# Expert rows by indirect DMA for the first 128 tokens of a mixture layer, up products for the other 384

## The chip, the cores and the metric

The kernel runs as one program on one core of a Trainium2 chip. The metric is the device time of that program in microseconds (us), the median of several runs. The engines are TensorE (PE, with its weight loads shown apart as PEld), VectorE (DVE), ScalarE (ACT), GpSimd (POOL) and SyncE (SP). SP and POOL also issue the transfers between device memory and SBUF.

## What is computed

The program is a two-layer diffusion-style block, then a block with sparse and dilated attention, then a product-key expert layer ("peer"). Only the expert layer is touched. For 512 tokens of 1024 features it computes:

```
q   = (xt @ w_q).reshape(T, H, 2, 64)                 # H = 8 heads
s   = einsum('thcd,cnd->thcn', q, subkeys)            # 2 x 128 subkeys
s1, i1 = top_k(s[:, :, 0], 16);  s2, i2 = top_k(s[:, :, 1], 16)
sc, ci = top_k(s1[..., :, None] + s2[..., None, :], 16)   # of 256 candidates
idx = e1 * 128 + e2                                   # 16 experts of 16384 for each head
g   = softmax(sc)
a   = einsum('cd,chkd->chk', x, u[idx])               # u, v: 16384 x 1024
out = einsum('chk,chkd->cd', gelu(a) * g, v[idx])
```

So each token has 128 experts (8 heads of 16). The kernel before does not pick rows of u at all: it multiplies every token with all 16384 rows of u, and the weights g, spread over a dense table of 16384 experts by 512 tokens that is zero except at the chosen ones, do the picking.

## The kernel before, in words

Numbers are float32. Each product on TensorE is made of three: weights and activations are each split into a high part in a reduced form of float32 (fp32r) and the rest (`hi`, `lo`), and hi*hi, lo*hi and hi*lo are summed in PSUM (`mm3`, line 322). A tile of weights of 128 outputs comes by DMA from SP's queue (`wunit`, line 282), ACT writes `wh` (line 276), DVE writes `wl` (line 277). `lin2` (line 1096) runs the 24 products of one such tile, 8 chunks of features by 3, each with 512 tokens as moving columns.

The expert layer is `peer`. Its parts, in the order in which the code names them:

- the queries and scores: 8 tiles of `wpq`, then the scores of head h are copied to `SCO` (line 1629).
- `route(b)`, b = 0 to 3, for 128 tokens each: on DVE, the best 16 of 128 scores for each head and half (lines 1639 to 1643), the best 16 of 50 candidates, softmax (ACT for the exponential), and the two expert indices e1 and e2 (lines 1680 to 1699). Three transposes on PE (line 1704) put them and the weights on partitions by pair.
- `weights(tb, share)`, tb = 0 to 31, for 16 tokens each: groups of four tokens. DVE makes two one-hot tables (line 1719); ACT scales one of them by g, high part and low part, in eight small operations (line 1728), or in one group of three of the last block DVE does it in two (line 1725). Four products of 256 columns (line 1732) give, for each token, the 128x128 table of its expert weights, high part and low part next to each other; ACT copies the low parts (line 1735), DVE adds (line 1736) into `gst`. After 16 tokens `gst` goes to the table `G` in device memory from POOL's queue (line 1738).
- `up(e, ahead)`, e = 0 to 127: the product of one tile of 128 rows of u with all 512 tokens (`lin2`), gelu on ACT (line 1763), and, when it is made ahead of its use, a store to device memory (`GA`, line 1766).
- the down part, 16 groups of 8 tiles: `gt`, the weights of 1024 experts for all tokens, comes from `G` (line 1781), the gelu tiles come back from `GA` (line 1787), DVE multiplies them (line 1791), ACT and DVE split them into `hid` (lines 1794, 1795), and eight `lin2` with tiles of v (2048 + 1024 products in all) are added to the output (line 1799).

The code writes an interleaving by hand: `routing()` yields the time that each step is thought to take on DVE and ACT, and whenever 3.62 us have gathered on either, one `up` is written (lines 1769 to 1776). `route(b + 1)` is written between the groups of `weights` of block b. By that count 121 of the 128 up products are written during the routing, and seven in the first group of the down part. A planner of the framework then fixes each engine's order from the written order and from what it takes to be ready; at run time each engine runs its list in order.

One-hot tables and scaled tables have two buffers (`NOH`), split weights three (`NWH`), PSUM tiles of 1024 columns two (`acc`).

Of the kernel before, what the change touches and what calls it, by code (L numbers as in the profile page):

```python
# [5 lines left out]
F32 = mybir.dt.float32  # L6
# [64 lines left out]
NOH = 2  # L71
# [7 lines left out]
SHARE = 3  # L79

# [102 lines left out]
def pack2(i, o):  # L183
# [33 lines left out]
    o["pu"] = i["peer_u_2"].reshape(128, 128, 8, 128).transpose(1, 3, 2, 0)  # L217
    o["pv"] = i["peer_v_2"].reshape(128, 16, 8, 8, 128).transpose(1, 3, 0, 2, 4)
# [25 lines left out]
class K:  # L244
# [26 lines left out]
    def split(self, raw, shape):  # L271
        """hi, lo of raw"""
# [12 lines left out]
    def take(self, key, hold=False):  # L285
        """the next weights of the plan, the ones behind them on their way; held ones stay until they are dropped"""
# [12 lines left out]
    def drop(self, w):  # L299
        """a held one that is used for the last time"""  # L300
        self.held -= 1
        self.refill(1)
        return w
# [13 lines left out]
    def mm3(self, outs, w, x, start, stop):  # L317
        """outs: psum aps; w: (hi, lo) stationary; x: per out (hi, lo) moving."""
# [20 lines left out]
    def ones_mean(self, src, n, dim):  # L339
        """mean over features of src [128, n] (sum over partitions / dim), as psum [128, n]"""  # L340
# [23 lines left out]
    def setup(self):  # L364
# [4 lines left out]
        # gains times -1/2, the weights of the gated convolution times 1/2  # L369
# [26 lines left out]
    def load_xc(self):  # L396
        """the context's tokens, three feature chunks to a tile"""
# [36 lines left out]
    def adv(self, n=1000):  # L434
        """n steps of the first of the generators that run beside the tasks"""
# [25 lines left out]
    def mod_group(self, l, g, ws):  # L461
        """columns 256 g to 256 g + 256 of the modulation of layer l"""
# [15 lines left out]
    def mods(self, todo):  # L478
        """closures for the groups (layer, group) of todo; a group's weights are loaded behind the group before it"""
# [8 lines left out]
    def tick(self, upto=1000):  # L488
        """one more group of modulations, upto that many in all"""
# [4 lines left out]
    def mod_fold(self, l, j, gname, plus_one, k0, k1):  # L494
        """[128, k1 - k0, 2]: -gain / 2 * (mod_j (+1))"""
# [1374 lines left out]
```

## Time and profile before

| | us |
|---|---|
| median of 3 runs | 3798.35 (3797.68 to 3798.63) |
| the profiled execution, first to last instruction | 3799.5 |
| routing, weights and up products (2322 to 3098.8) | 776.8 |
| down part (3098.8 to the end) | 700.7 |

| engine, whole span | busy us | share |
|---|---|---|
| PE | 3700.0 | 97% |
| DVE | 2464.8 | 65% |
| ACT | 1749.5 | 46% |
| POOL | 159.3 | 4% |

The stage limits are read from the first and last starts of instructions: the products of `hid` start at 3098.8. Consecutive products on PE overlap in the records, so the pace of a kind is the distance between starts, not the duration of one. The same holds for DVE and ACT, where one instruction's end overlaps the next one's start by about 0.1 us.

### The profile page before, as it was taken

How to read it: one execution, taken by the hardware profiler on the slowest of the kernel's cores; microseconds unless marked ns; L12 is line 12 of the kernel's file. 1: busy time of each engine (PE TensorE's matmuls, PEld its weight loads, DVE VectorE, ACT ScalarE, POOL GpSimd, SP SyncE). 2: the span in 40 equal slices, each digit the busy share in tenths (PEclk: the TensorE clock that was granted, in tenths of full speed). 3: DMA queues.
4: the chain of work that ended last, by engine and by line, in shares of the span. 5: the costliest groups of instructions: out<-in, count | busy, mean ns of one | idle time of the engine just before them, and what ended most of it. 6: DMA issues, size and time to landing. Idle time of an engine off the chain costs nothing.

```text
span 3799.5 us, 52788 instructions
## 1 busy us (share of the span) xinstructions
PE 3700.0 (97%) x19762; PEld 3052.0 (80%) x19762; DVE 2464.8 (65%) x4950; ACT 1749.5 (46%) x3452; POOL 159.3 (4%) x317
## 2 busy tenths in 40 slices
PE   8998999999999999999999999999999999999999
PEld 5867788888877878887778878778888888888887
DVE  5966644444788655555776568999666855555554
ACT  5256531111446732233565544767777743322232
POOL 0000000000000000000001100000000011111110
PEclk9999999999999999999999999999999999999999
DMA  6430331222341233334331233455555565665553
GB/s 209 129 106 12 122 117 62 61 66 63 105 147 51 67 117 95 94 97 138 115 99 62 93 111 106 156 168 176 178 178 178 195 218 189 201 205 187 190 186 114
DMA packets 155248, 490.28 MB, mean 129 GB/s; under 512 B 18368, under 2 KB 24832, under 8 KB 150768
## 3 DMA queue, kind: packets, MB, share of 16 engines
q1 hardware_dynamic: 128368, 374.48, 30.9%
q0 software_dynamic: 26624, 112.43, 8.7%
q8 instruction: 156, 2.56, 0.3%
q14 instruction: 100, 0.82, 0.1%
HBM read 408.86 MB, written 74.71 MB: 127 GB/s over the span
## 4 chain that ended last, share of the span: by engine, by line
PE 85%; DVE 9%; ACT 2%; DMA 2%; issue 1%; SPq 0%; POOL 0%; ACTq 0%; DVEq 0%; POOLq 0%
PE b L322 56%; PE a L322 19%; PE b L917 2%; DVE wl L277 1%; PE b L467 1%; PE a L1732 1%; PE b L568 1%; PE b L906 1%; PE b L1419 1%; PE b L1365 1%; DMA mraw<-in_wmod_dram 1%; DVE gst L1736 1%; PE a L1125 0%; PE b L1507 0%; PE b L1174 0%
## 5 line engine op out<-in xcount | busy, mean ns | idle before, releaser
L276 ACT CAST wh<-raw 128x1024 fp32r<-128x1024 f32 (+2 forms) x531 | 547.3, 1031 | 1365.7 <-PE b L322 811.3
L322 PE MATMUL b<-hs,wh 128*128 128x512 f32 x2624 | 823.6, 395 | 4.4 <-ACT hs L1092 4.4
L277 DVE TENSOR_TENSOR wl<-raw,wh 128x1024 fp32r<-128x1024 f32 (+2 forms) x531 | 635.7, 1198 | 171.7 <-ACT wh L276 159.1
L322 PE MATMUL b<-hid,wh 128*128 128x512 f32 x2048 | 630.7, 389 | 0.0
L322 PEld LDWEIGHTS b<-hs,wh 128*128 128x128 f32 x2624 | 487.5, 190 | 107.7 <-ACT hs L1092 5.3
L322 PE MATMUL b<-hs,wl 128*128 128x512 f32 x1312 | 516.2, 393 | 1.1 <-DVE wl L277 1.1
L322 PEld LDWEIGHTS b<-hid,wh 128*128 128x128 f32 x2048 | 384.4, 188 | 80.2 <-DVE hid L1795 0.3
L322 PE MATMUL b<-hid,wl 128*128 128x512 f32 x1024 | 398.3, 389 | 0.0
L322 PE MATMUL b<-hh,wh 128*128 128x256 f32 (+1 forms) x1160 | 364.7, 351 | 3.7 <-DVE V L840 2.2
L322 PE MATMUL a<-hh,wh 128*128 128x512 f32 (+1 forms) x1144 | 354.7, 348 | 9.5 <-DVE y L1046 7.2
L322 PE MATMUL b<-hl,wh 128*128 128x256 f32 (+1 forms) x1160 | 356.3, 344 | 0.3 <-DVE hl L534 0.3
L322 PE MATMUL b<-hh,wl 128*128 128x256 f32 (+1 forms) x1160 | 355.7, 344 | 0.0
L322 PE MATMUL a<-hh,wl 128*128 128x512 f32 (+1 forms) x1144 | 350.2, 344 | 1.5 <-DVE wl L277 1.5
L322 PE MATMUL a<-hl,wh 128*128 128x512 f32 (+1 forms) x1144 | 349.9, 343 | 0.3 <-DVE hl L534 0.3
L322 PEld LDWEIGHTS b<-hs,wl 128*128 128x128 f32 x1312 | 248.4, 189 | 53.7 <-DVE wl L277 1.5
L322 PEld LDWEIGHTS b<-hh,wh 128*128 128x128 f32 x1160 | 200.5, 189 | 44.0 <-issue 4.7
L322 PEld LDWEIGHTS a<-hh,wh 128*128 128x128 f32 x1144 | 197.0, 188 | 44.3 <-issue 14.0
L322 PEld LDWEIGHTS b<-hl,wh 128*128 128x128 f32 x1160 | 201.0, 189 | 30.5 <-issue 1.2
L322 PEld LDWEIGHTS b<-hid,wl 128*128 128x128 f32 x1024 | 192.2, 188 | 39.9
L322 PEld LDWEIGHTS a<-hl,wh 128*128 128x128 f32 x1144 | 197.3, 188 | 31.8 <-issue 2.5
L322 PEld LDWEIGHTS b<-hh,wl 128*128 128x128 f32 x1160 | 200.4, 189 | 27.7 <-issue 1.1
L322 PEld LDWEIGHTS a<-hh,wl 128*128 128x128 f32 x1144 | 196.9, 188 | 30.3 <-DVE wl L277 2.3
(412 smaller groups left out, 5424.1 us busy)
## 6 DMA issues: line engine op xcount, KB each, us to landing
raw<-in_w_dram SPq DMA_DIRECT2D x134, 512.0 KB
raw<-in_pu_dram SPq DMA_DIRECT2D x128, 512.0 KB
raw<-in_pv_dram SPq DMA_DIRECT2D x128, 512.0 KB
raw<-in_win_dram SPq DMA_DIRECT2D x64, 512.0 KB
G<-gst POOLq DMA_DIRECT2D x32, 1024.0 KB, 4.9
gt<-G POOLq DMA_DIRECT2D x16, 2048.0 KB, 13.9
mraw<-in_wmod_dram SPq DMA_DIRECT2D x82, 384.0 KB
GA<-ga SPq DMA_DIRECT2D x121, 256.0 KB
```

The source lines that it names most:

```text
L276: nc.scalar.copy(hi, raw)
L277: nc.vector.tensor_tensor(lo, raw, hi, op=OP.subtract)
L322: nc.tensor.matmul(o, w[wi], xx[xi], start=start and xi == 0 and wi == 0, stop=stop and wi == 1)
L467: nc.tensor.matmul(p[j:j + 32, 0:256], self.cs[:, k, :], ws[k], start=k < 4, stop=k >= 4, tile_position=(0, j))
L568: nc.tensor.matmul(p[:, :w], self.ones[1024], s, start=k == 0, stop=k == 7)
L906: nc.tensor.transpose(p[:, j * 128:j * 128 + 128], Ps[e][:, kc * 128:kc * 128 + 128], self.eye)
L917: nc.tensor.matmul(o[pr, c % 2 * 128:c % 2 * 128 + 128], V[i][:, kc, pr], PT[e * nkb + kc], start=kc == 0, stop=kc == nkb - 1, tile_positi ...
L1365: nc.tensor.transpose(p[:, j * 128:j * 128 + 128], src, self.eye)
L1419: nc.tensor.matmul(o[row], V[kb][:, 128 * b + 64 * g:128 * b + 64 * g + 64], PT[kb][2 * g + b], start=False, stop=kb == qb and b == 1, til ...
L1732: nc.tensor.matmul(p[:, i * 256:i * 256 + 256], A[:, i], W[:, i].rearrange("p j e -> p (j e)"), start=True, stop=True)
L1736: nc.vector.tensor_tensor(gst[:, :, t8:t8 + 4].rearrange("p e t -> p t e"), q[:, :, 0], lo, op=OP.add)
```

## The change

For the first 128 tokens the up products are no longer made with all experts. After `route(0)` the flat expert index of each of the 128 pairs of each token is kept in `IDX`; `gather()` reads, for pair j, one row of u for each of the 128 tokens (128 rows of 4 KB, one indirect DMA on POOL's queue), and DVE multiplies that tile with the tokens (`XT`, token-major) and sums along the features into one column of `AU`. That is 128 DMAs and 128 DVE instructions of 128x1024. Three row buffers are used (`NGU`). Then gelu of `AU`, times g, and the result takes the place of g in the dense table of block 0.

The up products run on the other 384 tokens only. The order of the blocks becomes 1, 2, 3, 0, with `route(0)` and `route(1)` first, rows written alternately with the steps of `route(2)` and `route(3)`, the other rows beside and after the weights of block 3, and the weights of block 0 last, since they need `AU`.

In `weights` the high and low parts are now summed in PSUM: eight products of 128 columns for four tokens, where there were four of 256, and one ACT copy of 128x1024 for eight tokens, where there were two ACT copies of 128x512 and two DVE additions. In the down part the first 128 columns of a tile are copied from `gt` by ACT, and DVE multiplies the other 384.

```diff
+NGU = 3
+    o["un"] = i["peer_u_2"]
-    def lin2(self, ap, hs, shape=(128, 8, 128)):
+    def lin2(self, ap, hs, shape=(128, 8, 128), n=S):
-        p = self.acc1()
+        p = self.acc1()[:, :n]
...
+            if b == 0:
+                nc.vector.scalar_tensor_tensor(IDX, e12[:, 0], 128.0, e12[:, 1], op0=OP.mult, op1=OP.add)
+                nc.vector.tensor_copy(E0, e12)
+                nc.vector.tensor_copy(G0, gz)
+            else:
+                by_pair(b, e12, gz)
...
+        def gather():
+            ru = fr.enter_context(self.tc.tile_pool(name="ru", bufs=1))
+            AU = ru.tile([128, 128], F32, name="au")
+            XT = ru.tile([128, D], F32, name="XT")
+            U = {}
+            def issue(j):
+                U[j] = self.t("ug", [128, D], bufs=NGU, pool=ru)
+                nc.gpsimd.indirect_dma_start(out=U[j], out_offset=None, in_=a["un"],
+                                             in_offset=bass.IndirectOffsetOnAxis(ap=IDX[:, j:j + 1], axis=0))
+            for j in range(NGU - 1):
+                issue(j)
+            p = self.acc()
+            for k in range(8):
+                x = self.t("xs", [128, 128], bufs=2, pool=ru)
+                nc.vector.tensor_tensor(x, hs[k][0][:, :128].bitcast(F32), hs[k][1][:, :128].bitcast(F32), op=OP.add)
+                nc.tensor.transpose(p[:, k * 128:k * 128 + 128], x, self.eye)
+            nc.scalar.copy(XT, p)
+            yield 1500
+            for j in range(128):
+                u = U.pop(j)
+                nc.vector.tensor_tensor_reduce(u, u, XT, 1.0, 0.0, OP.mult, OP.add, AU[:, j:j + 1])
+                if j + NGU - 1 < 128:
+                    issue(j + NGU - 1)
+                yield 1150
+            nc.scalar.activation(AU, AU, AF.Gelu_apprx_tanh)
+            nc.vector.tensor_tensor(G0, G0, AU, op=OP.mult)
+            by_pair(0, E0, G0)
...
-                for i in range(4):
-                    nc.tensor.matmul(p[:, i * 256:i * 256 + 256], A[:, i], W[:, i].rearrange("p j e -> p (j e)"), start=True, stop=True)
-                q = p.rearrange("p (t j e) -> p t j e", t=4, j=2)
-                lo = self.t("glo", [128, 4, 128], bufs=1, pool=rt)
-                nc.scalar.copy(lo, q[:, :, 1])
-                nc.vector.tensor_tensor(gst[:, :, t8:t8 + 4].rearrange("p e t -> p t e"), q[:, :, 0], lo, op=OP.add)
+                    for i in range(4):
+                        c = 128 * (t4 + i)
+                        for j in range(2):
+                            nc.tensor.matmul(p[:, c:c + 128], A[:, i], W[:, i, j], start=j == 0, stop=j == 1)
+                nc.scalar.copy(gst[:, :, t8:t8 + 8], p.rearrange("p (t e) -> p e t", t=8))
...
+            for ns in route(1):
+                yield ns, 0
+            r0.close()
+            rows = gather()
+            def beside(r):
+                for ns in r:
+                    yield ns
+                    yield next(rows, 0)
-            for b in range(4):
-                r = route(b + 1) if b < 3 else iter(())
+            for b in (1, 2, 3, 0):
+                r = beside(route(b + 1)) if b in (1, 2) else rows if b == 3 else iter(())
...
-            p = self.lin2(a["pu"][e], hs)
+            p = self.lin2(a["pu"][e], [(hi[:, 128:], lo[:, 128:]) for hi, lo in hs], n=S - 128)
...
-                nc.vector.tensor_tensor(gv, gv, gt[:, :, e, :], op=OP.mult)
+                n0 = 128 // TBW
+                nc.scalar.copy(gv[:, :n0], gt[:, :n0, e, :])
+                nc.vector.tensor_tensor(gv[:, n0:], gv[:, n0:], gt[:, n0:, e, :], op=OP.mult)
```

## Rows read from the trace of the kernel before

**Rows 1.** The page's head: span; engine, busy us (share), instructions.

```profile
span 3799.5 us, 52788 instructions
PE 3700.0 (97%) x19762; PEld 3052.0 (80%) x19762; DVE 2464.8 (65%) x4950; ACT 1749.5 (46%) x3452; POOL 159.3 (4%) x317
```

**Rows 2.** Busy time by stretch; the header names the columns, x counts instructions.

```profile
core 0: us, PE busy (x) PEld busy (x) DVE busy (x) ACT busy (x) POOL busy (x), PEclk, DMA share, GB/s
2322.00:2400.00 78.00, 72.56 (x312) 59.33 (x311) 76.69 (x373) 34.26 (x66) 0.00 (x0) 0.96 0.40 119
2400.00:2500.00 100.00, 95.65 (x437) 79.20 (x436) 100.00 (x354) 69.97 (x172) 2.14 (x4) 0.97 0.49 166
2322.00:3099.00 777.00, 765.74 (x3573) 636.79 (x3572) 627.10 (x1540) 552.09 (x1354) 23.21 (x39) 0.99 0.53 177
3099.00:3796.00 697.00, 696.76 (x3073) 576.25 (x3072) 380.46 (x497) 203.33 (x248) 86.24 (x130) 1.00 0.57 182
```

**Rows 3.** Chain that ended last, in order of time: start us, us, what.

```profile
2537.64 5.48 PE b L322 x24
...
3063.83 5.57 DMA G<-gst
...
3069.95 13.42 DMA gt<-G
```

**Rows 4.** Where the top-16 searches, routing's last step and G's stores lie, by line.

```profile
L1639 DVE MAX8 tv<-sco x64: 272/288/334, 2272.8 to 2547.1; 128x8 f32<-128x128 f32 x64
...
L1699 DVE TENSOR_REDUCE e<-eq x32: 654/676/727, 2351.7 to 2772.2; 128x32 f32<-128x512 f32 x32
...
L1738 POOL DMA_DIRECT2D G<-gst x32: 532/532/542, 2412.8 to 3063.8; - x32
```

**Rows 5.** PE in order of time: fp32r products of 384 columns in attention.

```profile
2013.12 0.33 PE L1125 MATMUL a<-lo,qz 128*128 128x384 f32 x1
...
2014.16 0.34 PE L1125 MATMUL a<-lo,qz 128*128 128x384 f32 x1
```

**Rows 6.** PE in order of time: fp32r products of 256 columns at the start.

```profile
64.43 0.28 PE L322 MATMUL a<-hl,wh 128*128 128x256 f32 x1
...
64.90 0.28 PE L322 MATMUL a<-hh,wl 128*128 128x256 f32 x1
```

**Rows 7.** Weight loads of 32, 64 and 128 columns by line: ns min/median/max.

```profile
L467 PEld LDWEIGHTS b<-mraw,cs x656: 106/109/177, 37.3 to 1355.4; 128*32 128x32 f32 x164
...
L917 PEld LDWEIGHTS b<-PTq,V x832: 132/137/232, 201.3 to 1282.5; 128*64 128x64 f32 x167
...
L1732 PEld LDWEIGHTS a<-ohW,ohA x512: 186/188/288, 2388.0 to 3059.2; 128*128 128x128 f32 x171
```

**Rows 8.** DVE in order of time in the last block of weights.

```profile
3010.07 1.22 DVE L277 TENSOR_TENSOR wl<-raw,wh 128x1024 fp32r<-128x1024 f32 x1
3011.21 1.04 DVE L1736 TENSOR_TENSOR gst<-a,glo 128x512 f32<-128x512 f32 x1
...
3015.91 0.69 DVE L1725 TENSOR_TENSOR ohW<-ohB,ghT 128x512 fp32r<-128x512 f32 x1
3016.51 1.06 DVE L1736 TENSOR_TENSOR gst<-a,glo 128x512 f32<-128x512 f32 x1
3017.41 0.68 DVE L1725 TENSOR_TENSOR ohW<-ohB,glT 128x512 fp32r<-128x512 f32 x1
```

**Rows 9.** ACT in order of time in the last block of weights.

```profile
3009.61 0.58 ACT L1735 COPY glo<-a 128x512 f32<-128x512 f32 x1
3010.07 1.28 ACT L1728 ACTIVATE ohW<-ohB,ghT 128x128 fp32r<-128x128 f32 x4
3011.25 0.98 ACT L1728 ACTIVATE ohW<-ohB,glT 128x128 fp32r<-128x128 f32 x3
```

**Rows 10.** Whom DVE waited for, 2322 to 3064: us in total, times, longest.

```profile
DVE ohA L1719 <- PE a L1732: 66.0, 52, 3.8
DVE ohB L1719 <- ACT ohW L1728: 35.7, 39, 1.4
```

**Rows 11.** DMA issues of the page: KB each, median us to landing.

```profile
G<-gst POOLq DMA_DIRECT2D x32, 1024.0 KB, 4.9
...
ga<-GA POOLq DMA_DIRECT2D x121, 256.0 KB, 4.8
```

**Rows 12.** Landing times over all transfers of G's stores, then of GA's.

```profile
DMA to landing us min/median/max: 4.1/4.9/6.7
...
DMA to landing us min/median/max: 2.8/4.8/13.7
```

More of the change, by code (lines that the diff above doesn't have):

```diff
@@ L1616, in peer @@
         SCO = {}
+        r0 = __import__("contextlib").ExitStack()
+        rs = r0.enter_context(self.tc.tile_pool(name="rs", bufs=1))
         for h in range(8):
@@ L1627, in peer @@
                 if h % 2 == 0:
-                    SCO[b, h // 2] = self.t("sco", [128, 512], F32, 16, rt)
+                    SCO[b, h // 2] = self.t("sco", [128, 512], F32, 8, rs if b < 2 else rt)
                 nc.scalar.copy(SCO[b, h // 2][:, 256 * (h % 2):256 * (h % 2) + 256], p[:, 256 * b:256 * b + 256])
-        ET = [rt.tile([128, S], F32, name=n) for n in ("e1T", "e2T", "gT")]
+        ET = [rt.tile([128, S], F32, name=n) for n in ("e1T", "e2T")]
         GT = [rt.tile([128, S], F32R, name=n) for n in ("ghT", "glT")]
@@ new lines, in by_pair @@
+            nc.vector.tensor_tensor(GT[1][:, cs], gT, GT[0][:, cs], op=OP.subtract)
+        IDX = rt.tile([128, 128], U32, name="idx")
+        E0 = rt.tile([128, 2, 128], F32, name="e0")
+        G0 = rt.tile([128, 128], F32, name="g0")
+        def gather():
[25 more added lines that the diff above has]
+            by_pair(0, E0, G0)
@@ new lines, in weights @@
+            for t8 in range(0, TBW, 8):
+                p = self.acc()
+                for t4 in range(0, 8, 4):
+                    t0 = tb * TBW + t8 + t4
+                    A, B = (self.t(n, [128, 4, 128], F32R, NOH, rt) for n in ("ohA", "ohB"))
+                    W = self.t("ohW", [128, 4, 2, 128], F32R, NOH, rt)
+                    for o, e in ((A, ET[0]), (B, ET[1])):
+                        nc.vector.tensor_tensor(o, iota[:, None, :].to_broadcast([128, 4, 128]),
+                                                e[:, t0:t0 + 4, None].to_broadcast([128, 4, 128]), op=OP.is_equal)
+                    dve = share and (t0 // 4) % share == 0
+                    for j in range(2):
+                        g = GT[j].bitcast(F32)
+                        if dve:
+                            nc.vector.tensor_tensor(W[:, :, j], B.bitcast(F32), g[:, t0:t0 + 4, None].to_broadcast([128, 4, 128]), op=OP.mult)
+                        else:
+                            for i in range(4):
+                                nc.scalar.activation(W[:, i, j], B[:, i].bitcast(F32), AF.Copy, scale=g[:, t0 + i:t0 + i + 1])
+                    yield (2400, 0) if dve else (1200, 2350)
+                    for i in range(4):
+                        c = 128 * (t4 + i)
+                        for j in range(2):
+                            nc.tensor.matmul(p[:, c:c + 128], A[:, i], W[:, i, j], start=j == 0, stop=j == 1)
+                nc.scalar.copy(gst[:, :, t8:t8 + 8], p.rearrange("p (t e) -> p e t", t=8))
+                yield 0, 1100
@@ L1786, in peer @@
                     ga = self.t("ga", [128, S], bufs=NGA, pool=rg)
-                    nc.gpsimd.dma_start(out=ga, in_=GA[8 * g + e])
+                    nc.gpsimd.dma_start(out=ga[:, 128:], in_=GA[8 * g + e])
                 else:
```

39 lines of the change are left out of this document (12 added, 27 removed).

## The prediction

> **What bounds the kernel now.** I read the busy shares first: PE is busy 97% of the span, DVE 65%, ACT 46% [rows 1]. A change pays only where it takes time off PE, or it costs where it makes PE wait. Next I read busy time by stretch. The change lies in the stage from 2322 to 3098.8 us, 776.8 us long; there PE is busy 765.7, DVE 627.1, ACT 552.1 [rows 2]. In the down part behind it PE has no gap to speak of (696.8 of 697), so nothing that the change does on DVE or ACT there matters while they have half their time free [rows 2].
>
> The chain of the work that ended last shows the stage as pieces of 5.48 us, one tile of up products each [rows 3]: 128 x 5.48 = 701, plus 512 weight products of 256 columns. These start about 0.12 us apart ((64.90 - 64.43) / 4 [rows 6]): 61. Together 763, so PE loses some 14 us in the stage. It loses nearly all of it at the start, where DVE is full: from 2322 to 2500 DVE is busy 176.7 of 178 us and PE lacks 9.8 us, 5.5% [rows 2].
>
> Last I read which engine runs ahead. The routing of block 3 should by the written order lie beside the weights of block 2; but the top-16 searches end at 2547 and the last step of routing at 2772, while G's stores run from 2413 to 3064 [rows 4]. So the planner pulls VectorE's work forward wherever VectorE would be free. What counts for DVE is its total over the stage, not the place where the code writes a step.
>
> **What the change takes from PE.** An up tile is still 24 products, now of 384 columns. Six such steps took 2014.16 - 2013.12 = 1.04 us, 0.173 us each [rows 5], where 512 columns take 5.48 / 24 = 0.228. A tile becomes 4.18 us (I count 0.174), 128 tiles 535 us: 166 us less.
>
> The weight products become 1024 of 128 columns. The trace has no fp32r product of 128 columns. A line through 0.12 at 256 and 0.173 at 384 gives 0.065 as the low end. No gain over 256 columns, 0.12, is the high end. Weight loads speak for the upper part: 109, 137 and 188 ns for 32, 64 and 128 columns [rows 7], 0.82 ns for each column, so 128 columns occupy the loading path about 0.105 us, and each product has its own load. I take 0.11: 113 us, 51 more than now (ends 67 and 123).
>
> PE's work in the stage is then 535 + 113 = 648 us, 114 less than 763.
>
> **What it does to DVE.** The 128 additions into `gst` go. One occupies 3017.41 - 3016.51 = 0.90 us [rows 8]: 115 us less. 128 multiply-and-sum instructions of 128x1024 come. The trace has none; the nearest row is the two-input subtraction of the same shape, 3011.21 - 3010.07 = 1.14 us [rows 8]. I take that, 146 us. Below it the end is 1.05, the same less a start-up; above it 2.28, if the sum needed a second pass. The eight additions for `XT`, the index and the products for block 0 are some 3 us. The seven last tiles of the old stage already took DVE work of the down part, 14 instructions of 0.6 us, 8 us, which now lies behind the stage. Sum: 627 - 115 + 146 + 3 - 8 = 653 us. DVE keeps its work and PE loses 114: the two are now level. That is the main thing.
>
> **What it does to ACT.** Two copies of 512 (0.46 us each [rows 9]) become one of 1024, about 0.9 by twice the row; gelu gets a quarter shorter. ACT stays near 550. In the down part ACT gets 128 copies of 128 columns, no more than its 0.3 us small operations [rows 9], 38 us beside 494 free; no cost, since PE sets the pace there. If that cover were gone it would be those 38 us.
>
> **What it does to POOL and the transfers.** 128 more DMAs of 512 KB, 67 MB, in a stage that now moves 177 GB/s at a share of 0.53 [rows 2], which is 334 GB/s if all were in use. The stage moves 137 MB now; with 67 more and 8 MB less of `GA` it would be about 196 MB in 740 us, 265 GB/s, share 0.8. It fits but no longer with room. POOL's queue also carries G's stores: a gather behind a store waits until ACT has written `gst`. Behind each row instruction on DVE stand the splits `wl` and the one-hot tables, and behind those PE; a late gather stops all three. A transfer of half a megabyte should land between the best of 256 KB, 2.8, and the worst of 1 MB, 6.7; the median of either is 4.9 [rows 11, 12]. With three buffers a row can be had every (4.9 + 1.14) / 3 = 2.0 us (ends 1.3 and 2.6). 128 rows need 256 us of a stretch of over 500, so I cost them at nothing beyond DVE's work; not hidden, 25 rows left at the end at 2.0 us would cost 50 us.
>
> One rule of the Trainium skill speaks against this: GPSIMD Engine Reference, section 8 (Key points), says that GpSimd shares its SBUF interfaces with VectorE and that the two contend when a VectorE instruction has two SBUF inputs, which nearly all of them here have. This trace does not show it for plain transfers: POOL's issue of G's stores lasted 532 to 542 ns over all 32 [rows 4], and they landed in 4.1 to 6.7 us [rows 12], while DVE was busy from a half to all of the time.
>
> **The end of the stage is new.** By the steps that the code counts, all 128 up tiles are now written before the weights of block 0 (11 and 12 with the two first routings, 38, 38 and 29 with blocks 1, 2 and 3); today seven are left over and cover the way from the last G to the first `hid`. So two stretches lose their cover.
>
> The weights of block 0: 21 groups with eight ACT operations of 1.18 / 4 = 0.295 us [rows 9] are 50 us, 16 copies of 0.9 are 14: 64 us. DVE needs 64 x 0.6 + 22 x 0.6 = 52 beside it [rows 8]. PE has 256 x 0.11 = 28 of that. Block 0 can begin only when all rows are done.
>
> Then G's last store, the load of `gt` and the first tiles: 5.6 + 13.4 [rows 3], 0.7 between and behind them, and then eight `hid` at two DVE instructions of 0.6 [rows 8], 9.6 us, where PE would need 5.5: about 26 us in all, in which PE stands.
>
> **The sum.** Before the last block PE has 648 - 28 = 620 us, DVE 653 - 52 = 601. With DVE as full as that I give PE the loss that it has today where DVE is full, 5.5%: 620 / 0.945 = 656 us. Then 64 + 26 = 90. Stage: 746 against 776.8, 31 less. The profiled span of 3799.5 is 1.2 above the median of 3798.35, so the median goes to about 3798 - 31 = 3767; I add 3 for the start of the gathers, whose first indices come only with the end of the first routing: 3770 us.
>
> **The rivals.** First, VectorE becomes the bound (slower). It has 601 us in the 656, in order, with waits behind PE and ACT (66.0 and 35.7 us today [rows 10]) and new ones behind gathers. Today it idles 150 of 777 us in this stage, 19.3%, at no cost. Kept at that share the stretch would last 601 / 0.807 = 745, the stage 835, the median 3856. The point from which it decides: the stretch may last 687 until nothing is left of the gain, an idle share of DVE of 12.5%. For it speaks the level sum; against it that DVE ran at 99% from 2322 to 2500. Chance 0.24.
>
> Second, gathers are slow (slower): POOL's descriptors held up by VectorE, or transfers queueing. At the worst landing of the trace, 13.7 us [rows 12], a row comes every (13.7 + 1.14) / 3 = 4.9 us, 633 us from about 2416 on, 727 from the stage's start; with 90 the stage is 817, the median 3838. Chance 0.06, since G's stores show nothing of it.
>
> Third, the planner mixes block 0 into the up tiles, because the rows are ready early (128 at 2.0 us are done by about 2700 if DVE has room). Then most of the 36 us that PE stands in the last block are gone: 3730 to 3740. Chance 0.10. Against it: DVE has hardly any room.
>
> Fourth, losses of 679 to 694 in the first stretch cancel the gain: within 0.2%, 3791 to 3806. Chance 0.13.
>
> That the up products don't become shorter is excluded by the rows of 384 columns.
>
> **How the numbers follow.** The forecast (3740 to 3790) has 0.47. Faster is that and the third rival: 0.57; same 0.13; slower 0.30. 0.2%, 7.6 us, is about what a measurement can tell from no change. The range: at the low end the first stretch has only 10 us of loss (630) and the first `hid` come as soon as `gt` has landed (21): 715, 3737, and a little of the third rival, 3733; at the high end the first rival at its full price, 3856. Weight products at 0.065 would free PE but not DVE and add nothing below that; a second pass in the sum (146 us more on DVE) would go beyond the top and I leave it out.
>
> **What the profile should show.** Up tiles in the chain of 4.2 us; weight products 0.11 apart; row instructions of 1.2 us whose wait for gathers is small; DVE above 90% busy up to the last block; PE nearly idle in the last block and for 20 us behind it. I am wrong if DVE waits long for rows, if the rows of `AU` end well behind the last up tile, or if block 0 is spread among the up tiles.

## The result, and the profile after

| | us |
|---|---|
| before, beside it on the same chip | 3798.01 (3796.28 to 3798.63, 4 runs) |
| after | 3884.26 (3882.83 to 3888.24, 4 runs) |
| ratio | 1.0228, 95% interval 1.0214 to 1.0243 |

The change makes the kernel 86 us slower. The forecast was 3770, its range ended at 3856.

First the page's head (it answers to [rows 1]): VectorE has hardly more work than before, TensorE has less, and yet the span is 81 us longer.

```profile
span 3880.8 us, 54259 instructions
PE 3662.9 (94%) x20282; PEld 3122.1 (80%) x20282; DVE 2478.0 (64%) x5090; ACT 1759.2 (45%) x3518; POOL 321.2 (8%) x452
```

Then busy time by stretch, as in [rows 2]. The limits are the first row instruction (2439), the last one (2885), the last up tile (3066) and 3181, where the chain below leaves the first tiles of the down part; the first product of `hid` starts 12 us before that, at 3169.8.

```profile
core 0: us, PE busy (x) PEld busy (x) DVE busy (x) ACT busy (x) POOL busy (x), PEclk, DMA share, GB/s
2322.00:2439.00 117.00, 107.18 (x607) 104.38 (x606) 115.58 (x479) 47.69 (x79) 3.10 (x3) 0.97 0.54 167
2439.00:2885.00 446.00, 368.66 (x2057) 358.84 (x2058) 384.94 (x944) 273.74 (x665) 163.91 (x141) 0.90 0.85 288
2885.00:3066.00 181.00, 180.97 (x1119) 180.32 (x1120) 87.64 (x105) 141.00 (x349) 6.50 (x12) 0.99 0.59 198
3066.00:3181.40 115.40, 74.09 (x301) 66.17 (x301) 67.57 (x109) 76.37 (x213) 15.35 (x22) 0.54 0.40 137
3181.40:3880.00 698.60, 692.23 (x3035) 568.13 (x3033) 358.60 (x489) 220.85 (x358) 82.86 (x126) 1.00 0.53 170
```

Two holes in TensorE stand out. While rows are gathered it lacks 77 of 446 us, with the transfers at a share of 0.85; VectorE is not full there either (it lacks 61). Behind the last up tile it lacks 41 of 115, at a granted clock of 0.54. Between the two, from 2885 on, the rows are done and TensorE is full: that stretch runs as forecast.

What did VectorE wait for in the 446 us? The view of waits (us in total, times, longest) has in effect one answer, the gathers (all its other rows together are 4.2 us). The same view of TensorE names whom that held up.

```profile
DVE ug L1754 <- DMA ug<-in_un_dram,idx: 56.8, 40, 5.5
```

```profile
PE b L324 <- DVE wl L279: 26.7, 11, 5.0
PE a L1786 <- DVE ohA L1772: 23.9, 12, 5.2
PE a L1786 <- ACT ohW L1781: 15.3, 6, 7.5
```

VectorE in order of time shows one such wait. The row instruction stands 3.44 us for its gather; a one-hot table and the split `wl` of a tile of u stand behind it in the list and start only when it and the next row are through.

```profile
2799.90 0.69 DVE L1772 TENSOR_TENSOR ohB<-iota,e2T 128x512 fp32r<-128x512 f32 x1
2804.02 1.23 DVE L1754 CUSTOM_DVE_ANT_0 ug<-ug,XT 128x1024 f32<-128x1024 f32 x1 [3.44 <-DMA ug<-in_un_dram,idx]
2805.17 0.08 DVE L1754 DVE_READ_ACCUMULATOR2_ANT au<- 128x1 f32 x1
2805.71 1.23 DVE L1754 CUSTOM_DVE_ANT_0 ug<-ug,XT 128x1024 f32<-128x1024 f32 x1 [0.45 <-DMA ug<-in_un_dram,idx]
...
2806.86 0.69 DVE L1772 TENSOR_TENSOR ohB<-iota,e2T 128x512 fp32r<-128x512 f32 x1
2807.46 1.22 DVE L279 TENSOR_TENSOR wl<-raw,wh 128x1024 fp32r<-128x1024 f32 x1
```

All instructions that touch the row buffers (ns min/median/max, first and last start), and what GpSimd's gathers sat idle for:

```profile
L1740 POOL DMA_INDIRECT ug<-in_un_dram,idx x128: 937/1147/1903, 2374.3 to 2877.2; - x128
L1754 DVE CUSTOM_DVE_ANT_0 ug<-ug,XT x128: 1197/1217/1262, 2439.3 to 2884.7; 128x1024 f32<-128x1024 f32 x128
its engine sat idle before it (us, times) until:
  DVE au L1754: 286.4, 96
```

A row comes every (2884.7 - 2439.3) / 127 = 3.5 us. 96 of the 128 gathers are issued only when a row instruction has freed their buffer, and VectorE waits 40 times for what they bring: each engine waits for the other in turn.

ScalarE has a new wait too. In the same 446 us it stands for tiles of u that have not landed (first line); in the kernel before it does not do so there at all, and in the kernel without gathers of the experiments once (second line).

```profile
ACT wh L278 <- DMA raw<-in_pu_dram: 41.8, 9, 11.3
```

```profile
ACT wh L278 <- DMA raw<-in_pu_dram: 4.3, 1, 4.3
```

The longest of these waits can be followed back. A tile of u has three buffers (`raw`), and SP asks for the next tile when VectorE's `wl` has read an old one out.

```profile
2859.41 1.21 DVE L279 TENSOR_TENSOR wl<-raw,wh 128x1024 fp32r<-128x1024 f32 x1
2860.65 0.33 SPq L284 DMA_DIRECT2D raw<-in_pu_dram  x1
2869.11 1.05 ACT L278 CAST wh<-raw 128x1024 fp32r<-128x1024 f32 x1 [11.33 <-DMA raw<-in_pu_dram]
```

ScalarE had stood since 2857.8; the tile was asked for at 2860.65 and was there 8.5 us later. The `wl` in front of it is the split of a tile whose `wh` ScalarE had finished at 2843.4: it came 16 us later, behind seven row instructions that waited 7.6 us for gathers. So the late rows also hold up the loads of u.

Last the chain of work that ended last, for the sizes of the steps (as [rows 3]):

```profile
2877.16 6.40 DMA ug<-in_un_dram,idx
...
2927.40 4.25 PE b L324 x24
...
2946.90 1.74 PE a L1786 x16
...
3081.39 0.90 ACT gst L1787
...
3084.10 1.77 PE a L1786 x7
...
3148.43 4.16 DMA G<-gst
...
3155.79 12.28 DMA gt<-G
```

### The profile page after: what moved, and what is told of

Its sections match the earlier page's. It is cut to its first block, busy times and chain, and to the rows that moved or that the text cites. A ratio compares the mean times of both kernels' runs of the same rounds, so it can differ in the third digit from the quotient of the medians.

```text
span 3880.8 us, 54259 instructions
## 1 busy us (share of the span) xinstructions
PE 3662.9 (94%) x20282; PEld 3122.1 (80%) x20282; DVE 2478.0 (64%) x5090; ACT 1759.2 (45%) x3518; POOL 321.2 (8%) x452
## 4 chain that ended last, share of the span: by engine, by line
PE 61%; issue 18%; DVE 11%; DMA 4%; ACT 3%; POOL 3%; SPq 0%; POOLq 0%; ACTq 0%; DVEq 0%
PE b L324 32%; PE a L324 18%; DVE wl L279 2%; DMA ug<-in_un_dram,idx 2%; PE b L919 2%; POOL ug L1740 2%; PE b L469 1%; POOL ga L1848 1%; PE a L1786 1%; PE b L570 1%; DVE ug L1754 1%; PE b L908 1%; PE b L1421 1%; ACT ohW L1781 1%; PE b L1367 1%
## 5 line engine op out<-in xcount | busy, mean ns | idle before, releaser
L324 PE MATMUL b<-hs,wh 128*128 128x384 f32 (+1 forms) x2624 | 735.0, 361 | 5.5 <-ACT hs L1094 4.4
L324 PE MATMUL b<-hs,wl 128*128 128x384 f32 (+1 forms) x1312 | 470.2, 358 | 29.3 <-DVE wl L279 29.3
L1786 PE MATMUL a<-ohW,ohA 128*128 128x128 f32 x1024 | 169.0, 318 | 66.7 <-ACT ohW L1781 30.7
L1786 PEld LDWEIGHTS a<-ohW,ohA 128*128 128x128 f32 x1024 | 161.9, 232 | 77.9 <-ACT ohW L1781 59.7
```

The source lines that it names most:

```text
L324: nc.tensor.matmul(o, w[wi], xx[xi], start=start and xi == 0 and wi == 0, stop=stop and wi == 1)
L1786: nc.tensor.matmul(p[:, c:c + 128], A[:, i], W[:, i, j], start=j == 0, stop=j == 1)
```

## The experiments

Differences below are medians against the kernel before, measured beside each on the same chip. A ratio's interval is some 0.15 to 0.3% to either side, so a difference of two runs is good to some 10 to 15 us.

**The two parts that save or cost TensorE time, without rows.** First the up products of 384 columns alone, in the old order:

```diff
 before.py
-            p = self.lin2(a["pu"][e], hs)
+            p = self.lin2(a["pu"][e], [(hi[:, 128:], lo[:, 128:]) for hi, lo in hs], n=S - 128)
```

> The kernel before with another part alone: up products of 384 columns, and no expert rows at all for the first 128 tokens (their up products are left out, so their expert output is wrong; the weights and the order of the blocks are those of before). TensorE has 166 us less. If the saving reaches the end as far as VectorE's 619 us in the stage allow: a stage of 640 to 660, 3660 to 3685. If VectorE, now the bound, keeps its idle share of 19%: a stage of 765, 3785.

3675.5 against 3796.06, ratio 0.9679 (0.9651 to 0.9707): 121 us less, where the shorter tiles alone are worth 128 x (5.48 - 4.25) = 157. VectorE's busy time suggests where the rest is lost:

```profile
2500.00:2800.00 300.00, 284.91 (x1648) 278.53 (x1647) 292.84 (x767) 262.78 (x687) 8.50 (x16) 0.98 0.57 195
```

With TensorE's work shortened VectorE is busy 293 of 300 us in the middle of the stage, and TensorE lacks 15. That the full VectorE is the reason is not shown; the run with both parts, below, speaks against it.

Then the new `weights` alone in the kernel before:

```diff
 before.py, weights()
-                    nc.tensor.matmul(p[:, i * 256:i * 256 + 256], A[:, i], W[:, i].rearrange("p j e -> p (j e)"), start=True, stop=True)
+                        for j in range(2):
+                            nc.tensor.matmul(p[:, c:c + 128], A[:, i], W[:, i, j], start=j == 0, stop=j == 1)
...
-                nc.vector.tensor_tensor(gst[...], q[:, :, 0], lo, op=OP.add)
+                nc.scalar.copy(gst[:, :, t8:t8 + 8], p.rearrange("p (t e) -> p e t", t=8))
```

> The kernel before with one part of the change alone: the weight products of 128 columns with both parts summed in PSUM, one copy on ScalarE for eight tokens, no additions on VectorE. By the sum of the prediction TensorE gets 51 us more and is the bound there: 3840 to 3850. If 128 columns cost in proportion (0.065 us): 3805. If the 115 us that leave VectorE matter more: below 3798.

3858.6 against 3796.06, ratio 1.0161 (1.0131 to 1.019): 62 us more. The chain shows what a product of 128 columns costs beside up tiles of 512:

```profile
2655.29 0.84 PE a L1735 x8
2656.13 5.50 PE b L322 x24
```

0.84 / 8 = 0.105 us, the same as the 0.82 ns for each of 128 columns that [rows 7] gave for the loads. 1024 of them are 107.5 us where the 512 of before are 61, 47 more. Of the other 15 some 6 lie in the first stretch, where TensorE now lacks 16 of 178 us (9.8 before, [rows 2]); the rest is within the uncertainty:

```profile
2322.00:2500.00 178.00, 161.77 (x750) 134.80 (x749) 178.00 (x825) 101.14 (x229) 2.15 (x4) 0.94 0.41 136
```

So 115 us less on VectorE brought nothing by themselves and cost TensorE in full. (The edit also shortens the times that the written order counts, so 16 of the 128 up tiles, not seven, now lie in the down part; the same holds for the next run.) Both together (the two edits above):

> The kernel before with the two parts that were run alone, up products of 384 columns and the new weight products, and no rows; blocks in the old order, so the last up products still cover the way to the down part as far as they are left over. The expert rows of the first 128 tokens are left out. If the parts add: 3796 - 121 + 62 = 3737. If VectorE, 115 us lighter, lets more of the up products' saving through: 3715 to 3730. The distance to the run without rows in the new order is then the price of that order: 60 to 85 us, if the uncovered end of the stage is what I think.

3735.78 against 3797.63, ratio 0.9831 (0.9802 to 0.9859): 62 us less; the parts add up (-121 + 62 = -59). So the 115 us taken off VectorE let no more of the up products' saving through. VectorE is now busy 207 of the 300 us that it filled above, and TensorE lacks 13 of them as it lacked 15:

```profile
2500.00:2800.00 300.00, 286.76 (x1767) 283.18 (x1767) 207.19 (x480) 253.48 (x642) 8.01 (x15) 0.98 0.52 181
```

**The order and the end, without rows.** The kernel after without gathers, row instructions and their gelu; the time steps that the written order counts for them stay:

```diff
 after.py, gather()
-            for j in range(NGU - 1):
-                issue(j)
...
-                nc.vector.tensor_tensor_reduce(u, u, XT, 1.0, 0.0, OP.mult, OP.add, AU[:, j:j + 1])
...
+            for j in range(128):
+                yield 1150
```

> The changed kernel without the rows altogether: no gathers, no row instructions, nothing multiplied into the weights of block 0, but the same written order of blocks and the same number of up products at each place. The expert rows of the first 128 tokens are left out. It shows what is left when the rows cost nothing: by the run without gathers (3824) less the loss that VectorE's 146 us of rows still bring. Theory A (the rows' work on VectorE holds TensorE up too): 3785 to 3800. Theory B (only the gathers did, and the end of the stage costs its 115 us anyway): 3815 to 3824.

3789.2 against 3797.63, ratio 0.9978 (0.9966 to 0.999): 8 us less. Against the run with both parts in the old order that is 53 us lost to the new order alone. It lies at the end, where no up tile is left to cover block 0 and the way to `hid` (the second stretch below, from the last up tile to the first product of `hid`):

```profile
2500.00:2800.00 300.00, 286.82 (x1747) 285.26 (x1746) 186.34 (x426) 217.73 (x524) 6.94 (x13) 0.98 0.52 182
...
2982.00:3081.00 99.00, 62.05 (x258) 57.13 (x258) 56.90 (x90) 66.71 (x192) 8.64 (x12) 0.50 0.36 129
```

**The rows' work without their transfers.** One fixed tile `U0` of u is loaded once and multiplied 128 times; nothing is gathered:

```diff
 after.py
-                nc.gpsimd.indirect_dma_start(out=U[j], out_offset=None, in_=a["un"],
-                                             in_offset=bass.IndirectOffsetOnAxis(ap=IDX[:, j:j + 1], axis=0))
...
-                nc.vector.tensor_tensor_reduce(u, u, XT, 1.0, 0.0, OP.mult, OP.add, AU[:, j:j + 1])
+                nc.vector.tensor_tensor_reduce(u, U0, XT, 1.0, 0.0, OP.mult, OP.add, AU[:, j:j + 1])
```

> The changed kernel without its 128 gathers: one tile of 128 rows of u is loaded once and every row instruction multiplies that tile (two scratch buffers for its product), so the work on VectorE stays and the transfers, GpSimd's issues and the waits for them go. The expert rows of the first 128 tokens are left out. Theory 1 (VectorE is simply full: routing and rows are put ahead of the splits that TensorE needs, and waits for gathers only stand in for waits that would come anyway): 3860 to 3884. Theory 2 (the gathers: VectorE stands 57 us for them between 2439 and 2885, with TensorE behind it, and the transfers delay the weights too): 57 us or more come off, 3815 to 3830.

3823.64 against 3796.06, ratio 1.0078 (1.0055 to 1.01): 28 us more than before, 36 more than without any row work, 59 less than the whole change. Now VectorE is full in the middle of the stage, and there it waits 0.5 us in all:

```profile
2500.00:2800.00 300.00, 269.46 (x1568) 263.58 (x1567) 299.50 (x755) 208.52 (x503) 6.39 (x12) 0.94 0.48 161
```

That is the whole sum: both parts -62, order and end +53, the rows' work on VectorE +36, the gathers +59, together +86.

**What of a gather costs the 59 us?** If it were VectorE's time, less work there would help. The gathers are kept, each row instruction reads the first 64 of 1024 features:

```diff
 after.py
-                nc.vector.tensor_tensor_reduce(u, u, XT, 1.0, 0.0, OP.mult, OP.add, AU[:, j:j + 1])
+                nc.vector.tensor_tensor_reduce(u[:, :64], u[:, :64], XT[:, :64], 1.0, 0.0, OP.mult, OP.add, AU[:, j:j + 1])
```

> The changed kernel with all gathers, but each row instruction multiplies only the first 64 of 1024 features, so 128 instructions fall from 1.14 to about 0.15 us and 127 us leave VectorE. The rest of the sum over features is left out. Theory 1 (VectorE's work): the stretch of the rows shortens by 80 us or more, about 3800. Theory 2 (the pace of the gathers, 3.5 us each with three buffers, sets the stretch): 128 rows still take about 400 us, VectorE waits 150 us or more for them, and no more than 30 us come off: 3855 or more.

3895.74 against 3796.06, ratio 1.0259 (1.0229 to 1.0288): no faster (13 us slower, at the edge of the uncertainty). VectorE's waits in the 446 us, and then the busy times of that stretch (columns as above):

```profile
DVE ug L1754 <- DMA ug<-in_un_dram,idx: 134.4, 66, 7.0
```

```profile
2439.00:2885.00 446.00, 354.34 (x1962) 343.16 (x1962) 266.32 (x952) 269.56 (x662) 146.18 (x141) 0.88 0.81 281
```

VectorE's work fell by 119 us, its waits for gathers rose from 57 to 134, and TensorE got even less done (354 for 369). The rows themselves did get faster: with so little to do VectorE takes one every 2.8 us, the last at 2797 instead of 2885. But the denser gathers cost TensorE more, 89 of the 358 us that the rows now last, for 77 of 446. So with gathers on, the loss is theirs and not that of VectorE's work. Then half the bytes: rows of the first 512 features (2 KB), each multiplied twice, so that VectorE's elements stay the same:

```diff
 after.py
-    o["un"] = i["peer_u_2"]
+    o["un"] = i["peer_u_2"][:, :512]
...
-                U[j] = self.t("ug", [128, D], bufs=NGU, pool=ru)
+                U[j] = self.t("ug", [128, 512], bufs=NGU, pool=ru)
...
-                nc.vector.tensor_tensor_reduce(u, u, XT, 1.0, 0.0, OP.mult, OP.add, AU[:, j:j + 1])
+                nc.vector.tensor_tensor_reduce(u, u, XT[:, 512:], 1.0, 0.0, OP.mult, OP.add, AH)
+                nc.vector.tensor_tensor_reduce(u, u, XT[:, :512], 1.0, 0.0, OP.mult, OP.add, AU[:, j:j + 1])
```

> The changed kernel with all 128 gathers, each of only the first 512 features of its rows (2 KB a row, 33 MB for 67); the row instruction becomes two of 512, so VectorE's work stays. The other half of the sum is left out. If the bytes of the gathers, on top of the weights' own, make them late (share 0.9 where they run), the waits for them, 57 us, nearly go, and the time falls towards that without gathers: 3825 to 3845. If it is a fixed time for each gather (issue on GpSimd, descriptors, the way to landing): 3870 or more.

3855.29 against 3795.57, ratio 1.0157 (1.0132 to 1.0182): 27 us of the 59 are gone. The gathers' landing times, and the busy times of the stretch:

```profile
DMA to landing us min/median/max: 3.3/4.2/8.3
```

```profile
2439.00:2885.00 446.00, 387.57 (x2195) 377.73 (x2195) 404.72 (x1209) 282.40 (x678) 159.19 (x141) 0.92 0.69 226
```

The share of the transfers falls to 0.69 and VectorE's waits for gathers to 32 us. About half of the price goes with the bytes, the other half does not. (Two row instructions of 512 start 0.60 us apart where one of 1024 takes 1.14, so VectorE has some 8 us more to do here, and the part that does not go may be smaller by that.)

**More buffers.** Four row buffers; for room, four buffers of `GA` tiles instead of six:

```diff
 after.py
-NGU = 3
+NGU = 4
-NGA = 6
+NGA = 4
```

> The changed kernel with four row buffers for three, paid for with four buffers for six of the gelu tiles. If a gather's time from issue to landing (5 to 10 us) sets the pace of the rows, a row comes every 2.6 us where it came every 3.5, and 30 to 54 us come off: 3830 to 3855. If the transfers' bandwidth sets it (share 0.85 to 0.9 in that stretch), the landings only get longer: 3875 to 3884.

3878.01 against 3797.63, ratio 1.0205 (1.0175 to 1.0235): 6 us less, within the uncertainty. The edit was not clean, and only the trace parts its two halves. The first product of `hid` starts at 3149.4, 20 us earlier than after (3169.8); the down part then takes 731.5 us instead of 711.0, and there TensorE waits for `hid` 29 times, which it hardly does after (3.3 us). Up to `hid` the fourth buffer is worth 20 us; VectorE's waits for gathers halve (first fence), the transfers are now at a share of 0.91 (second, a stretch within the rows), and TensorE pays in the down part (third, its waits from 3150 on):

```profile
DVE ug L1754 <- DMA ug<-in_un_dram,idx: 30.4, 25, 2.7
```

```profile
2700.00:2800.00 100.00, 87.70 (x518) 86.36 (x516) 94.92 (x176) 78.22 (x198) 41.89 (x38) 0.93 0.91 324
```

```profile
PE b L324 <- DVE hid L1858: 19.2, 29, 0.9
```

**Rows spread out.** My theory then was that the rows come too densely: the planner takes all 128 in 446 us. This kernel ties each pair of indices to the gelu of an up tile (the product with 0.0 makes it wait), 1.7 rows for each tile from the 24th on:

```diff
 after.py
+                if j % 2 == 0:
+                    nc.vector.scalar_tensor_tensor(IDX[:, j:j + 2], LAST[0][:, 128:130], 0.0, IDF[:, j:j + 2], op0=OP.mult, op1=OP.add)
...
+                if ROWS[0]:
+                    CR[0] += RPU
+                    while CR[0] >= 1:
+                        CR[0] -= 1
+                        next(ROWS[0], None)
```

> The same work as the changed kernel, in another order: 1.7 rows are written behind each up product from the 24th on, and the indices of each two rows are made by a small VectorE instruction that also reads that product's gelu, so the planner cannot put the rows ahead of it. Rows no longer count in the rule that places up products, so 19 of these stand beside the weights of block 0 and six in the down part. If the loss comes from all rows being pulled into 440 us (transfers at 0.9, VectorE full, TensorE starved there) and from the uncovered end, both go: a stage of 690 to 740, 3715 to 3765. If the rows' amount of work and transfers is the loss wherever they lie, only the cover of the end helps, as in the run with 4.40 us: 3840 to 3870.

3935.78 against 3795.57, ratio 1.0365 (1.0341 to 1.039): 54 us worse than after. The transfers are relieved (share 0.66 from 2439 to 3140). The gathers' landing times, then VectorE's and TensorE's waits in that stretch:

```profile
DMA to landing us min/median/max: 4.0/6.2/10.0
```

```profile
DVE ug L1759 <- DMA ug<-in_un_dram,idx: 175.3, 85, 5.8
...
PE a L1791 <- DVE ohA L1777: 110.8, 33, 9.8
```

Landing takes as long as in the dense kernel below (5.9 in the middle). ScalarE's waits for tiles of u nearly go (2.9 us for 41.8). But an index that is ready late shows VectorE the whole landing time, 175 us of it, and TensorE waits 111 us behind that. The theory falls for rows that are spread in this way: drawing them forward, as the planner did, hides more than it costs. Rows that are spread without such a tie were not tried.

**The old weights in the changed kernel.** Products of 256 columns and additions on VectorE are put back; for room, five `GA` buffers:

```diff
 after.py, weights()
-                        for j in range(2):
-                            nc.tensor.matmul(p[:, c:c + 128], A[:, i], W[:, i, j], start=j == 0, stop=j == 1)
+                    nc.tensor.matmul(p[:, i * 256:i * 256 + 256], A[:, i], W[:, i].rearrange("p j e -> p (j e)"), start=True, stop=True)
...
-NGA = 6
+NGA = 5
```

> The changed kernel with the weight products, copies and additions of before (256 columns, additions on VectorE), one part undone; five gelu buffers for six, to make room. TensorE gets 51 us less, VectorE 115 more. If the parts simply add, as they did without rows (-62): 3820. If VectorE bounds the stretch of the rows, the additions lengthen it, 64 of them lie there: 3870 to 3920.

3841.92 against 3795.57, ratio 1.0121 (1.0097 to 1.0146): 40 us better than after, with 115 us more on VectorE. The gathers' landing times, VectorE's waits from 2439 to 2885, and the busy times from 2600 to 2800, here and after:

```profile
DMA to landing us min/median/max: 4.1/5.9/9.7
```

```profile
DVE ug L1754 <- DMA ug<-in_un_dram,idx: 15.0, 9, 4.1
```

```profile
2600.00:2800.00 200.00, 186.50 (x1054) 182.54 (x1053) 195.68 (x482) 148.18 (x371) 47.45 (x40) 0.95 0.78 259
```

```profile
2600.00:2800.00 200.00, 169.79 (x956) 166.34 (x955) 185.87 (x467) 121.74 (x291) 80.20 (x69) 0.91 0.90 308
```

A landing is long, but VectorE waits for it 15 us instead of 57 (21 over all rows), since it has the additions to do between the rows, and TensorE is busy 93% from 2600 to 2800 where it was 85% after. The price of this order shows at the end: the last gather goes out at 3008 instead of 2877 and the last row is read at 3015, behind the last up tile (2996), so from there to the first product of `hid` (3124.2) it takes 128 us where it took 104 after.

**Covering the end.** The time after which an up tile is written is raised from 3.62 to 4.40 us, which leaves 15 tiles for block 0 and 4 for the down part:

```diff
 after.py
-PEER_NS = 3620
+PEER_NS = 4400
```

> The changed kernel with one number changed: an up product is written for each 4.40 us of VectorE's or ScalarE's time, not 3.62. By the code's own count 15 up products then stand beside the weights of block 0 and four in the down part; before all 128 stood ahead of it. If the uncovered end (115 us with TensorE's clock at 0.54) is a loss of its own, 19 x 4.25 = 81 us of work move into it: 3800 to 3820. If VectorE sets the time throughout, nothing is won: 3870 or more.

3865.79 against 3797.63, ratio 1.0173 (1.0143 to 1.0202): 18 us better than after. The end is covered (TensorE is busy 73 of the 84 us from 3066 to 3150, and `hid` starts at 3150.5), but the tiles are now missing earlier: TensorE lacks 21.5 of 117 us before the rows (9.8 after), 77 beside them as before, and 5.6 more behind them.

The same with the old weights (both edits above):

> The change with the weights part of the kernel before (four products of 256 columns, copies on ScalarE, additions on VectorE; NGA 5 for room) and PEER_NS 4400 instead of 3620, so that some 15 up tiles are written beside block 0 and some 4 into the down part. Theory A (of the change's loss, part is the costlier weight products and part the uncovered end; the gathers' price stays): the two gains, 42 us of e_oldw and 18 us of e_ns4400, come together, and with fewer up tiles beside the rows no more than that: 3884 - 60 = 3825 us, 3810 to 3835, first product of hid near 3110 to 3120. Theory B (the end was the whole rest of the loss): 3842 less the 45 to 60 us in which TensorE hardly works between the last up tile and hid: 3780 to 3797, better than before. Theory C (up tiles moved to the end only move the loss into the stretch with the rows): 3842, 3836 to 3850.

3857.27 against 3796.97, ratio 1.0155 (1.0138 to 1.0172): 14 us worse than with the old weights alone, so neither do the two gains come together, nor was the end the whole rest. The first `hid` starts at 3149.8 instead of 3124.2. TensorE's waits, 2600 to 3000, here and then with the old weights alone:

```profile
PE b L1722 <- DVE e L1704: 54.7, 2, 35.8
```

```profile
PE b L1722 <- DVE e L1704: 21.4, 2, 17.4
```

The transposes of a routing stand in TensorE's list and wait for its last step on VectorE; with fewer up tiles written ahead of them TensorE comes there sooner and stands 33 us longer. No kernel here that does the whole work beats the one before.

## Why the prediction was wrong, step by step

**TensorE's own work: right.** An up tile was forecast at 4.18 us and takes 4.25 (128 tiles: 544 for 535). A weight product was taken at 0.11, from the weight loads, and takes 0.105 to 0.109 in the chain (8 in 0.84, 16 in 1.74; 107.5 to 112 for 113). Together some 654 where 648 was forecast. In the down part, which was forecast to cost nothing, TensorE lacks 6.4 of 698.6 us from 3181 on, 0.2 of 697 in the kernel before [rows 2].

**VectorE's and ScalarE's work: right.** The row instruction was taken at 1.14 us from the subtraction; two in a row start 1.14 to 1.15 apart, and the accumulator read of 0.08 overlaps the next. VectorE's busy time from 2322 to 3066 is 115.58 + 384.94 + 87.64 = 588 us for 601. The copy of 1024 columns has pieces of 0.90 in the chain, as taken.

**The first stretch: wrong, 744 us (2322 to 3066) for 656.** This is 88 of the 114 us missed (3884 - 3770); 24 more lie at the end and in the down part behind it. The term was 620 us of TensorE, divided by 0.945. The runs take it apart by the end of the last up tile. Without rows it ends at 2982, after 660 us: 5.5% were right for that kernel, with VectorE at 62% in the middle. With the rows' work but no transfers it ends at 3013, 691 us, VectorE at 99.8% from 2500 to 2800. With the gathers it ends at 3066. So two sizes failed:

- I had seen that the two engines were level, and gave TensorE the loss of a stage where only VectorE was full, and TensorE's list could run ahead of it later. The kernel before shows that VectorE's fullness was not what the 5.5% measured: in the 100 us behind the stretch that I took them from, VectorE is full as well and TensorE lacks 0.4.

  ```profile
  2500.00:2600.00 100.00, 99.63 (x471) 82.52 (x471) 100.00 (x312) 80.96 (x206) 2.14 (x4) 1.00 0.52 174
  ```

  With the rows' work on VectorE as well the stretch is 31 us longer than without, of the 88; that this is because each wait of one level engine is lost to the other is argued from it.
- "I cost them at nothing beyond DVE's work" for the gathers: 53 of the 88, and 59 in the whole. The pace of 2.0 us was worked out from a landing of 4.9 and three buffers alone. The landing is 5.9 in the middle and 9.7 at worst (measured with the old weights, the same bytes; the chain after has a gather of 10.3), and a buffer does not come back after landing and one instruction: the row instruction stands in VectorE's list behind splits and tables, and the next gather behind the row instruction. The three buffers together came back at 3.5 us a row.

The share of the transfers was forecast at 0.8 "in 740 us". I had read that the planner pulls VectorE's work forward wherever it is free [rows 4], and did not apply that to the transfers which hang on that work: all 128 rows came within 446 us, at 0.85, and 0.9 from 2600 to 2800. Halving the bytes gives back 27 us, so the bytes are part of the price. That the in-order wait (late rows in front of `wl` and the tables) is the other part is argued, from the waits that the traces show behind late rows and from the runs with 57, 134 and 175 us of waits for gathers, which took 3884, 3896 and 3936 us. How much of this part is GpSimd's issue, how much the landing, no run here separates. The loads of u suffer with it, and not by the bytes alone: at half the bytes and a share of 0.69 ScalarE still waited 58.6 us for tiles of u (41.8 after). The tiles that ScalarE waited for landed 4.0 to 9.0 us after they were asked for in the kernel after (eight of nine waits), 4.1 to 6.9 at half the bytes (13 of 14) and 5.2 in the one wait without gathers. So with whole rows some loads of u are slower, and in both kernels tiles are asked for late, behind a late `wl`; why there are more such waits at half the bytes stays open.

**The end: right in kind, 114 us for 90.** The lost cover is there: 104 us from the last up tile to the first product of `hid` (3066 to 3169.8), and the down part behind that takes 711.0 us where it took 700.7. Block 0 takes 82 us (to G's last store at 3148.4) for 64; the way from there to `hid`, 21, and the 10 more of the down part are 31 for 26. The 64 let ScalarE run through with TensorE's 28 us beside it. In the chain the products stand between ScalarE's steps: 7 products take 1.77 us at the granted clock of 0.54, where 8 took 0.84 before that; with two buffers of each table they are in series. The kernels without rows and without gathers have the same end (82 us for block 0 in both), so it is not the gathers' doing. That the clock is what stretched it is argued from the products' pace, not tried.

**The weights part: a price taken for a trade.** The forecast counted +51 us on TensorE and -115 on VectorE. The first came (47), the second was worth nothing: with the additions back the changed kernel is 40 us faster. In the changed kernel VectorE spent part of the freed time waiting for gathers (57 us for 15); but in the kernel before, where nothing is gathered, the 115 us bought nothing either.

**The rivals.** The first (VectorE's waits stretch the first stretch to 745, 3856 in all) has the right place and by chance the number, 744; VectorE idles 156 of 744 us, 21%, for the 19.3% that it supposed. But it put the loss down to VectorE's work and old waits; without gathers VectorE is as good as full and the loss is 35 us beyond the forecast's 656. The second, slow gathers, supposed 4.9 us a row; 3.5 were enough, since TensorE lost time beside the rows and not behind them. The truth lies between these two, and its end came 24 us dearer on top. The third did not come: block 0 begins behind the last up tile. Each rival was priced as if the others kept to the forecast; here two came together, and the range ended at one of them. Of the three signs of being wrong, one came: VectorE waits long for rows. The rows end well before the last up tile (2885 and 3066), and block 0 is not spread.

The contention rule that the prediction weighed (the Trainium skill, GPSIMD Engine Reference, section 8) is neither borne out nor refuted here. Issuing a gather takes GpSimd 1.147 us in the middle after and 0.938 where the row instructions read 64 features only, which agrees in direction; but it takes 0.960 in the last kernel above, whose row instructions read all 1024, and G's stores take 532 to 542 ns in the kernel without gathers, whose VectorE is full of such instructions. It is not what cost the time, since the kernel with the row instructions of 64 features was no faster. (That nearly all of VectorE's instructions have two inputs in SBUF was too much: the 128 additions, 115 us, read one of theirs from PSUM.)

## What to carry to other kernels

When a change makes two engines level, the loss of the old stage is no estimate for the new one: price every wait of either at its full length, and an indirect gather in front of an in-order engine at its worst landing, with the buffers' whole cycle (issue, landing, the place of its reader in the list), not the landing alone. Ask also which other loads get their buffers back from that list: they start late with it. If a planner pulls work forward, the transfers that hang on it come in that shorter time too: divide the bytes by that stretch, not by the stage. Time taken off an engine that waits for something else is worth nothing, and an operation moved to the bounding engine to get it costs in full.

## What the runs showed of the hardware

- An fp32r product of 128 columns with a weight load of its own takes 0.105 us, as much as its load (0.105, an estimate from the slope of [rows 7]); 256 columns take 0.12 [rows 6]. Two halves summed in PSUM cost TensorE 1.8 times one product of double width.
- An indirect gather of 128 rows of 4 KB lands in 4.0 to 10.0 us, 6 in the middle, at shares of 0.66 (spread rows) and 0.80 (old weights) alike; 128 rows of 2 KB in 3.3 to 8.3. Its issue holds GpSimd 0.94 to 1.9 us in the kernel after, a plain store of G there 0.53 to 0.59.
- The granted clock falls to 0.50 to 0.54, to or near the lower of its two levels (1.2 and 2.4 GHz), in the stretches behind the last up tile, in the kernels with rows and without. TensorE was full before it (181 of 181 us after, at 0.99) and works there in short pieces (62 of 99 us without rows); the clock is back at 1.00 in the down part.
